# One encoder block on one core: moving four small pieces of work between engines and within their queues

## The chip, the cores and the metric

The kernel runs on one core of one Trainium2 chip. The metric is the device time of one execution in microseconds (us). A core has TensorE (PE in the profile; its weight loads are listed apart, as PEld), VectorE (DVE), ScalarE (ACT), GpSimd (POOL) and SyncE (SP, which here only issues transfers). Each engine works through its own list of instructions in order. An instruction that has to wait for another engine holds up everything behind it on its own engine.

## The reference

The block computes, for 1024 tokens and 16 meta tokens put ahead of them (1040 columns in all), in float32:

```
h = h + mixer(rms_norm(h));  h = h + swiglu(rms_norm(h));  return rms_norm(h)[:, 16:]

mixer(h): q, k, v of branch A and of branch B and two gates are columns of h @ w_in
  branch A, per head (4):  s1 = q1 k1' * scale - slope * |i - j|   (meta keys have distance 0)
                           s2 = q2 k2' * scale - slope * |i - j|
                           y  = (softmax(s1) - lam * softmax(s2)) @ v, then rms_norm
  branch B: attention in a window of 128, with sinks
  merged = sigmoid(ga) * (y_a @ w_ba) + sigmoid(gb) * (y_b @ w_bb);  return merged @ w_o
```

## The kernel before

A float32 product is made of three matmuls on operands that are split into a high and a low part (`split`, lines 123 to 126: ACT makes the high part, DVE or POOL the low one). The large products use a scheme with 7 instead of 8 block products. The program goes through these stages: norms and projections with branch B's attention between them (to about 270 us), branch A's attention (270 to 590 us), the merge of the branches (from 603 us), the output product, and the feed-forward part (to the end). The change lies in branch A's attention and at the beginning of the merge.

**Branch A's attention** is a loop over 32 tiles (4 heads of 8 tiles of 128 query rows, numbered n = 0 to 31 here), with one more pass for what is left over. For each tile, `scores_a` makes two score maps of 128 x 1040, first m = 1, then m = 0. For each map PE multiplies in three chunks (line 1051): two of 352 columns into the two banks of the tile `two`, which has one buffer, and one of 336 into a bank of the tag `sc`, of which there are three. DVE reads the first two chunks in one instruction (line 1054), adding the distance and taking the row minimum, and then the third (line 1058). That one reads its distances from `far_m`, one of three small buffers that POOL fills by a copy from `dist` (`far_copy`, line 1001), one buffer for each tile in turn. ACT takes the exponential of a map (line 1062). DVE makes the reciprocal of a sum (1065), a factor (1067), and the combined map s1 - factor * s2 (1068, over 1040 columns). Behind that, line 1070 on DVE copies the 16 meta columns twice more to the right of the map (32 columns), because the value product later takes them in several roles.

One pass later `transpose_a` turns the map in three groups of blocks (b = 0, 1, 2; PE line 1080 into `sc` banks, ACT line 1083 and DVE line 1084 out of them; b = 2 is the group with the meta columns). `values_a` multiplies by the values (line 1093), and `normed_a` ends every fourth tile with a norm: its sums (line 1106) and its factors turned on PE (line 1117).

**The gates** run in the gaps of the attention. `gate_steps` yields after every three matmuls (line 938; three are called a quarter here, four quarters make one block product). The weights of a block product are made by POOL (`weights_g`, lines 817 to 837: up to two additions, then a cast at 836 and a subtraction at 837) into four buffers, four block products ahead. A buffer is free when PE has finished the block product that used it. Each result leaves PSUM by ACT or DVE (lines 945 to 977). The last column of gates (k = 7) has its block products p = 5, 7, 3, 4 last in the program; p = 4 goes on in the bank that p = 7's result has just been read from (line 970).

**The order on PE is written by hand.** A string of letters says what each pass does in turn: s is the next piece of scores (two chunk pieces and the last chunk for each map, six in all), t the next group of transposes, g one gate quarter, n the next piece of values or norm. Tiles from n = 16 on use `"ssgsgnssgtsgntgnt"`. For n % 4 = 3 the first n of that string is one of the empty waiting steps of `normed_a` (`N_WAIT`), so that there is no work in it. The other engines' orders come from a scheduler, which weighs readiness; `tc.issue_after(x)` makes it put what is inside behind x in order.

**At the merge** the results of branch B are loaded, and `split_yb` makes their high and low parts: `yb0` and `yb1` first (`ybpool`), then `yb2` and `yb3` (`ybpool2`), on ACT and DVE. Then come the products with `w_bb` (`branch_w` loads and splits their weights, line 742; the matmuls are at 750). Parts of `w_out`, 1 MB each, are loaded by `load_wo` (line 1340) in the same stretch.

Of the kernel before, what the change touches and what calls it, by code (L numbers as in the profile page):

```python
# [19 lines left out]
P = 128  # L20
# [6 lines left out]
NT = S // P  # L27
# [16 lines left out]
FAR_LATE = 6  # L44
LAST_B = ("T1", 4), (5, "V0"), (5, "T2"), ("T2", 6), (7, "V1"), (7, "V2")
SLOTS_LAST = "ggggntgntnt"
S_BUFS = (2, 2)
AT_BUFS = 2
G_BUFS = 3
# [29 lines left out]
def encoder_block(ctx: ExitStack, tc: tile.TileContext, x, meta, norm_mix, w_in, lq1, lk1, lq2, lk2,  # L79
# [656 lines left out]
    close_psum1()  # L736


    def branch_w(p, o, src, nme, raw=None, low=None, tag="wh"):
        w = (raw_tile(f"wbr{nme}_{o}")[:, 0:512] if raw is None else raw).rearrange("p (c n) -> p c n", n=P)  # L740
        if raw is None:
            nc.sync.dma_start(w, src[:, o * P:(o + 1) * P].rearrange("(c p) n -> p c n", p=P))
# [108 lines left out]
    def turn_into(i):  # L851
# [16 lines left out]
        if i == 2:  # L868
            for late in raws_g[4:]:
                queue_behind([late], last)  # L870

    def gate_steps():
        banks, kept = {}, {}

# [36 lines left out]
        for n, (k, p) in enumerate(order_g):  # L911
# [23 lines left out]
            for c in range(4):  # L935
# [6 lines left out]
                if c == 3:  # L942
# [18 lines left out]
                    elif p == 6:  # L961
                        u = kept.pop(k)
                        add(u, ps, u, ALU.add)
                        held_stores.append((u_d[k], u))
                    elif p == 5:
                        kept["q"] = kept_g(f"q_{k}")
                        nc.scalar.copy(kept["q"], ps)
                    elif p == 7:
                        st = stage_g(f"g22_{k}")
                        add(st, ps, kept.pop("q"), ALU.add)  # L970
# [25 lines left out]
    def far_copy(n):  # L996
        if n < AH * NT:
            with ExitStack() as after:
                if 2 < n < FAR_LATE:
                    after.enter_context(tc.issue_after(made_g[-1].ins))  # L1000
                nc.gpsimd.tensor_copy(far_m[n % 3][:, 0:S - 704], dist[:, 1600 - n % NT * P:1600 - n % NT * P + S - 704])

# [29 lines left out]
    def scores_a(h, t, ld, s):  # L1032
# [8 lines left out]
        u0 = 896 - t * P  # L1041
        far = far_m[(h * NT + t) % 3]
        for m in (1, 0):
            if m == 0:
                far_copy(h * NT + t + 2)
            s[m] = s0s[t % 2] if m == 0 else apool.tile([P, L], F32, tag="s1", name=f"as1_{nm}", bufs=S_BUFS[1])
            two = psum2.tile([P, 2, 512], F32, tag="two", name=f"aps2_{nm}_{m}", bufs=1)
            for i, (k0, n) in enumerate(A_CHUNKS):
# [18 lines left out]
        nc.vector.tensor_scalar(dn[:, 0:1], first_sum, dn[:, 1:2], neglam, ALU.mult, ALU.mult)  # L1067
        nc.vector.scalar_tensor_tensor(s[0][:, 0:L], s[1][:, 0:L], dn[:, 0:1], s[0][:, 0:L], ALU.mult, ALU.add)
        more, last = s[0][:, L:L + 2 * NM].rearrange("p (a k) -> p a k", a=2), s[0][:, S:L].unsqueeze(1).broadcast_to([P, 2, NM])
        nc.vector.scalar_tensor_tensor(more, last, 1.0, last, ALU.mult, ALU.max)  # L1070

    def transpose_a(h, t, s, at_):
        i = t % 2
# [85 lines left out]
    for n in range(AH * NT + T_LAG):  # L1159
# [30 lines left out]
            scoring = scores_a(h, t, ld, s)  # L1190
        if n >= T_LAG:
            turning = turn(tiles[n - T_LAG])
        for what in SLOTS[n % 2 if n < 2 * NT else 2] if n < AH * NT else SLOTS_LAST:
            if what == "s":
                next(scoring, None)
            elif what == "t":
# [54 lines left out]
    while n_made[0] < len(order_g):  # L1251
        fill(1)
    close_gwork()
    ybpool2, close_yb2 = pool("ybpool2")
    split_yb(ybpool2, 2)
    order_pe.__exit__(None, None, None)
    fill(1000)
    close_psum2()
    close_psumg()
    close_stage()  # L1260
# [95 lines left out]
    for o in range(DC):  # L1356
# [602 lines left out]
```

## Time and profile before

| | |
|---|---|
| median of 3 runs | 1411.83 us (1411.62 to 1412.45) |
| the profiled execution, its own time | 1410.71 us |
| its span, first to last instruction | 1408.9 us |
| outside the span | 1.81 us |
| PE busy | 1397.5 us, 99% of the span |
| DVE, ACT, POOL busy | 939.9, 673.9, 665.6 us |
| matmuls | 7171 |

A row of the trace's timeline gives the start of a group of equal instructions in us from the beginning of the span, the time from its start to the end of its last one, engine, line, operation, tiles (what is written, an arrow, what is read), shapes and count; in brackets stands the idle time of the engine ahead of it and what ended that. The matmuls of PE overlap in the trace: one of 512 columns is shown for 0.39 us, and the next starts 0.23 us after it. A stall shows in the distance of two starts, and only the part of it above 0.39 us is idle time of PE. A row of the waits gives who waited for whom, the total in us, how often, and the longest.

### The profile page before, as it was taken

What the parts mean: (1) busy time and instruction counts of PE and PEld (TensorE: products, weight loads), DVE (VectorE), ACT (ScalarE), POOL (GpSimd) and SP (SyncE); (2) the same over time, 40 slices, a digit from 0 to 9 for tenths busy, and PEclk for the clock granted to TensorE, in tenths of its full rate; (3) what the DMA queues carried; (4) which work ended last, traced back from release to release, by engine and by line L of the source; (5) the groups of instructions that cost most, each with busy time, mean ns of one, the idle gap of its engine ahead of it and who ended that gap; (6) DMA issues with size and microseconds to landing.
All of it is one profiled execution on the core that took longest, in us unless ns stands there. A gap on an engine that the chain in (4) does not pass through costs nothing.

```text
span 1408.9 us, 20675 instructions
## 1 busy us (share of the span) xinstructions
PE 1397.5 (99%) x7171; PEld 1199.4 (85%) x7171; DVE 939.9 (67%) x1619; ACT 673.9 (48%) x1285; POOL 665.6 (47%) x634
## 2 busy tenths in 40 slices
PE   9999999999999999999999999999999999999998
PEld 8989999888888888888888888888888888888886
DVE  6556667677677878767968956544455443887566
ACT  6356565545454555554446644333333333444454
POOL 4156885577777776523404055544444441000442
PEclk9999999999999999999999999999999999999999
DMA  8446658564886363495613634433233222954333
GB/s 238 91 123 181 199 177 295 148 194 155 266 286 221 109 202 107 140 323 160 202 43 120 187 110 139 133 112 110 96 101 108 102 99 107 367 181 141 120 126 146
DMA packets 193016, 227.73 MB, mean 162 GB/s; under 512 B 16952, under 2 KB 126464, under 8 KB 192784
## 3 DMA queue, kind: packets, MB, share of 16 engines
q1 hardware_dynamic: 190160, 222.80, 48.5%
q10 hardware_dynamic: 2752, 3.61, 0.8%
q8 instruction: 56, 0.92, 0.3%
q14 instruction: 48, 0.39, 0.1%
HBM read 152.48 MB, written 68.39 MB: 157 GB/s over the span
## 4 chain that ended last, share of the span: by engine, by line
PE 92%; DVE 4%; ACT 2%; issue 1%; POOL 1%; DMA 0%; SPq 0%; ACTq 0%; DVEq 0%; POOLq 0%
PE pg L1722 30%; PE pd L1826 15%; PE pg L938 9%; PE ppa L750 6%; PE po L1625 4%; PE aps L1051 3%; PE pp_va L236 3%; PE pp_ka L236 3%; PE pp_qb L236 3%; PE apy L1093 2%; PE bps L416 2%; PE pp_qa L236 2%; PE po L1633 2%; PE apt L1080 2%; PE bpy L463 1%; PE bpt L457 1%
## 5 line engine op out<-in xcount | busy, mean ns | idle before, releaser
L1722 PE MATMUL pg<-t,wop 128*128 128x512 f32 x1056 | 242.4, 389 | 0.0
L1722 PEld LDWEIGHTS pg<-t,wop 128*128 128x128 f32 x1056 | 198.2, 188 | 41.2
L125 POOL TENSOR_TENSOR wop<-wf,wop 128x512 fp32r<-128x512 f32 x114 | 151.2, 1326 | 164.8 <-ACT wop L124 152.8
L1826 PE MATMUL pd<-ob,oa 128*128 128x512 f32 x924 | 209.6, 389 | 0.0
L1826 PEld LDWEIGHTS pd<-ob,oa 128*128 128x128 f32 x924 | 173.4, 188 | 36.0
L938 PE MATMUL pg<-hT_hi,wopg 128*128 128x512 f32 x488 | 183.0, 401 | 0.8 <-POOL wopg L837 0.6
L1722 PE MATMUL pg<-b,wop 128*128 128x512 f32 x792 | 183.3, 389 | 0.0
L1722 PEld LDWEIGHTS pg<-b,wop 128*128 128x128 f32 x792 | 148.4, 188 | 30.7
L1062 ACT ACTIVATE as<-as,amn 128x1040 f32<-128x1040 f32 x64 | 74.6, 1166 | 99.5 <-DVE amn L1058 99.5
L124 ACT ACTIVATE wop<-wf 128x512 fp32r<-128x512 f32 x128 | 80.8, 632 | 73.3 <-PE pg L1722 49.7
L125 POOL TENSOR_TENSOR oa<-ra,oa 128x512 fp32r<-128x512 f32 x27 | 34.9, 1294 | 168.6 <-ACT oa L124 167.2
L938 PEld LDWEIGHTS pg<-hT_hi,wopg 128*128 128x128 f32 x488 | 91.5, 188 | 15.6 <-POOL wopg L837 1.1
L124 ACT ACTIVATE oa<-ra 128x512 fp32r<-128x512 f32 x77 | 48.7, 632 | 108.1 <-PE pd L1826 50.1
L938 PE MATMUL pg<-hT_lo,wopg 128*128 128x512 f32 x244 | 95.8, 393 | 0.0
L1499 DVE TENSOR_TENSOR s<-wf,wf 128x512 f32<-128x512 f32 x22 | 15.5, 704 | 111.2 <-DMA wf<-in_w_ff_up_dram 70.5
L1051 PE MATMUL aps<-ak,aq 128*128 128x352 f32 (+1 forms) x384 | 87.1, 335 | 1.9 <-DVE amn L1054 1.2
L1051 PEld LDWEIGHTS aps<-ak,aq 128*128 128x128 f32 x384 | 63.0, 189 | 11.8 <-DVE amn L1054 5.5
L1054 DVE CUSTOM_DVE_ANT_0 as<-aps,dist,far_a 128x704 f32<-128x704 f32 x64 | 60.3, 942 | 15.6 <-PE aps L1051 15.4
L418 DVE CUSTOM_DVE_ANT_0 bs<-bps,tbx,nsink 128x432 f32<-128x432 f32 (+1 forms) x64 | 38.5, 628 | 47.2 <-PE bps L416 32.6
L428 POOL TENSOR_SCALAR bs<-bs,bdn 128x432 f32<-128x432 f32 (+1 forms) x64 | 37.0, 596 | 51.9 <-DVE bdn L426 29.4
L1749 ACT COPY p<-pg 128x512 f32<-128x512 f32 x44 | 25.8, 587 | 66.5 <-PE pg L1722 66.5
L1093 PEld LDWEIGHTS apy<-at,av 128*128 128x128 f32 x400 | 54.0, 189 | 4.1
(340 smaller groups left out, 3164.1 us busy)
## 6 DMA issues: line engine op xcount, KB each, us to landing
ra<-aop SPq DMA_DIRECT2D x77, 256.0 KB, 2.6
wf<-in_w_ff_gate_dram SPq DMA_DIRECT2D x25, 512.0 KB, 3.7
wf<-in_w_ff_up_dram SPq DMA_DIRECT2D x25, 512.0 KB, 3.6
aop<-as SPq DMA_DIRECT2D x44, 256.0 KB, 2.1
wg_s<-in_w_in_dram SPq DMA_DIRECT2D x18, 512.0 KB, 4.5
aop<-c SPq DMA_DIRECT2D x33, 256.0 KB, 2.0
ak<-ka_d SPq DMA_DIRECT2D x16, 520.0 KB, 6.2
t_d<-tst SPq DMA_DIRECT2D x16, 512.0 KB, 4.5
```

Source lines behind the costliest of these rows:

```text
L124: high = nc.scalar.activation(hi, src, AF.Copy)
L125: lo_eng.tensor_tensor(lo, src, f32(hi), ALU.subtract)
L236: product = nc.tensor.matmul(ps[:, :n], a[:, c, :], b[:, c, at:at + n], start=(u == 0), stop=(u == 3 * DC - 1))
L750: nc.tensor.matmul(ps, w[:, a, j, :], src(j, b, tk), start=(j == 0 and n == 0), stop=(j == 3 and n == 2))
L938: product = nc.tensor.matmul(ps, op[:, x, c, :], h[:, 4 * d + c, HALF[t]], start=(p in (1, 6, 7) and c == 0 and i == 0), stop=(p in (2, 6, ...
L1051: nc.tensor.matmul(ps[:, :n], qs[m][:, t * P:(t + 1) * P], ks[m][:, vv, k0:k0 + n], start=(vv == 0), stop=(vv == 1))
L1054: nc.vector.tensor_tensor_reduce(s[m][:, 0:2 * n].rearrange("p (a k) -> p a k", a=2), two[:, :, :n], dist[:, u0:u0 + 2 * n].rearrange("p ( ...
L1062: nc.scalar.activation(s[m][:, 0:L], s[m][:, 0:L], AF.Exp, bias=mn[:, m, 1:2], scale=-1.0, accum_out=dn[:, 1:2] if m else first_sum)
L1093: nc.tensor.matmul(py[:, cols], v[:kp, a, k, :], at_[:kp, k, b, :], start=(k == 0 and j == 0), stop=(k == 8))
L1625: nc.tensor.matmul(sets_o[p][u], oa[:, a, u * P:(u + 1) * P], ob[:, b, :], start=(p in (1, 5) and j == 0 and k == 0), stop=(p in (2, 3) an ...
L1722: nc.tensor.matmul(ps, op[:, x, c, :], b[:, y, c, :], start=(p in (1, 5) and c == 0 and n == 0), stop=(p in (4, 2, 3) and c == 3 and n == ...
L1826: nc.tensor.matmul(ps[u], oa[:, a, u * P:(u + 1) * P], ob[:, b, :], start=(p in (1, 2, 5) and j == 0 and k == 0), stop=(p in (2, 3, 4) and ...
```

## The change

1. **Meta columns.** The copy of the 32 columns (line 1070) is no longer a `scalar_tensor_tensor` on DVE but a `copy` on ACT.
2. **Distance copies.** `far_copy` for tile n + 2 is called at the end of tile n, no longer between its two maps, and every copy from the fourth on is put in order behind the last gate weight that POOL was given by then (before, that held for three of them only).
3. **Fourth tiles.** Tiles 19, 23, 27 and 31 have an order string of their own, in which one gate quarter that stood behind the second map's two chunks stands ahead of them.
4. **Branch B's last parts.** The rest of the gates is written ahead of the split of `yb2` and `yb3`, and that split is put behind the addition that empties the last p = 7 bank. Three of the loads of `w_out` are put behind loads of `w_bb`.

```
+SLOTS_3 = "ssgsgngsstsgntgnt"
...
-            nc.sync.dma_start(w, ...)
+            w_loads[nme, o] = nc.sync.dma_start(w, ...)
...
-                        add(st, ps, kept.pop("q"), ALU.add)
+                        sums_g[k] = add(st, ps, kept.pop("q"), ALU.add)
...
-                if 2 < n < FAR_LATE:
+                if n > 2:
                     after.enter_context(tc.issue_after(made_g[-1].ins))
                 nc.gpsimd.tensor_copy(far_m[n % 3][:, 0:S - 704], dist[...])
...
         for m in (1, 0):
-            if m == 0:
-                far_copy(h * NT + t + 2)
...
-        nc.vector.scalar_tensor_tensor(more, last, 1.0, last, ALU.mult, ALU.max)
+        nc.scalar.copy(more, last)
+        far_copy(h * NT + t + 2)
...
-        for what in SLOTS[n % 2 if n < 2 * NT else 2] if n < AH * NT else SLOTS_LAST:
+        for what in (SLOTS_3 if n % 4 == 3 and n >= 2 * NT else SLOTS[n % 2 if n < 2 * NT else 2]) if n < AH * NT else SLOTS_LAST:
...
     close_gwork()
+    fill(1000)
     ybpool2, close_yb2 = pool("ybpool2")
-    split_yb(ybpool2, 2)
+    with tc.issue_after(sums_g[7].ins):
+        split_yb(ybpool2, 2)
     order_pe.__exit__(None, None, None)
-    fill(1000)
...
         if 3 <= o < 6:
-            load_wo(*((w11, 0, 0), (w12, 0, 1), (w21, 1, 0))[o - 3])
+            with tc.issue_after(w_loads["b", o].ins):
+                load_wo(*((w11, 0, 0), (w12, 0, 1), (w21, 1, 0))[o - 3])
```

Line numbers in the rows below are those of each kernel by itself: in the changed one they are 3 to 6 higher around here (line 938 is 943 there, 1054 is 1057, 1058 is 1061, 1062 is 1065, 1068 is 1071, 1080 is 1084, 1084 is 1088).

PE in tile 19, from the last chunk of its first map to the last chunk of its second (`aps` are scores, `pg` a gate quarter, `apt` the transposes), before:

```order
L1051 MATMUL aps_3_1_5571<-ak_1_5229,aq_1_5228 128x336 x2
L938 MATMUL pg_5_5481<-hT_hi,wopg_5_5391 128x512
L938 MATMUL pg_5_5481<-hT_lo,wopg_5_5391 128x512
L938 MATMUL pg_5_5481<-hT_hi,wopg_5_5391 128x512
L1051 MATMUL aps_2_3_0_5581<-ak_0_5234,aq_0_5233 128x352 x4
L938 MATMUL pg_5_5481<-hT_hi,wopg_5_5391 128x512
L938 MATMUL pg_5_5481<-hT_lo,wopg_5_5391 128x512
L938 MATMUL pg_5_5481<-hT_hi,wopg_5_5391 128x512
L1080 MATMUL apt_2_0_5592<-ident,as_0_3435 128x128 x4
L1051 MATMUL aps_3_0_5599<-ak_0_5234,aq_0_5233 128x336 x2
```

And now:

```order
L1054 MATMUL aps_3_1_5571<-ak_1_5229,aq_1_5228 128x336 x2
L943 MATMUL pg_5_5481<-hT_hi,wopg_5_5391 128x512
L943 MATMUL pg_5_5481<-hT_lo,wopg_5_5391 128x512
L943 MATMUL pg_5_5481<-hT_hi,wopg_5_5391 128x512 x2
L943 MATMUL pg_5_5481<-hT_lo,wopg_5_5391 128x512
L943 MATMUL pg_5_5481<-hT_hi,wopg_5_5391 128x512
L1054 MATMUL aps_2_3_0_5585<-ak_0_5234,aq_0_5233 128x352 x4
L1084 MATMUL apt_2_0_5591<-ident,as_0_3435 128x128 x4
L1054 MATMUL aps_3_0_5598<-ak_0_5234,aq_0_5233 128x336 x2
```

Three matmuls of a gate have moved from behind the second map's four matmuls to ahead of them, and the transposes follow these directly. PE's order differs at the same place of tiles 23, 27 and 31, and nowhere else.

DVE from the combined map of tile 27 to the first map of tile 28 (`as_1` is the map of tile 27; the bare rows of 128x1 read a minimum out), before:

```order
L1068 SCALAR_TENSOR_TENSOR as_1_3436<-as_3_3_6351,adn_3_6350,as_1_3436 128x1040
L1084 TENSOR_TENSOR at_2_6262<-apt_2_1_6410,at_2_6262 128x4x128
L1084 TENSOR_TENSOR at_2_6262<-apt_2_2_6432,at_2_6262 16x128
L1070 SCALAR_TENSOR_TENSOR as_1_3436<-as_1_3436 128x32
L1054 ISA as_3_4_6443,amn_4_6440<-aps_3_4_1_6444,dist,far_a 128x704
L1054 ISA amn_4_6440 128x1
```

And now:

```order
L1071 SCALAR_TENSOR_TENSOR as_1_3436<-as_3_3_6351,adn_3_6350,as_1_3436 128x1040
L1088 TENSOR_TENSOR at_2_6262<-apt_2_1_6409,at_2_6262 128x4x128
L1088 TENSOR_TENSOR at_2_6262<-apt_2_2_6431,at_2_6262 16x128
L1057 ISA as_3_4_6443,amn_4_6440<-aps_3_4_1_6444,dist,far_a 128x704
L1057 ISA amn_4_6440 128x1
```

The copy of the meta columns has gone from ahead of the next tile's first map, and the rest stands as it was. On ACT it stands now behind the last eviction of the transposes of tile 26 and ahead of the first exponential of tile 28:

```order
L1087 ACTIVATE at_2_6262<-apt_2_1_6409 128x4x128
L972 COPY q_6419<-pg_5_6301 128x512
L1087 ACTIVATE at_2_6262<-apt_2_2_6431 128x128
L1073 COPY as_1_3436<-as_1_3436 128x32
L1065 ACTIVATE as_3_4_6443,adn_4_6441<-as_3_4_6443,amn_4_6440 128x1040
L1087 ACTIVATE at_2_6262<-apt_3_0_6486 128x4x128
```

POOL in tiles 15 to 17 (`wopg` are gate weights being made, `far_m` with the numbers 3431, 3432 and 3433 are the three distance buffers), before:

```order
L836 CAST wopg_3_5072<-wg_s_0_4692 128x512
L837 TENSOR_TENSOR wopg_3_5072<-wg_s_0_4692,wopg_3_5072 128x512
L836 CAST wopg_4_5127<-wg_s_1_4690 128x512
L1001 COPY far_m_3431<-dist 128x320
L837 TENSOR_TENSOR wopg_4_5127<-wg_s_1_4690,wopg_4_5127 128x512
L824 TENSOR_TENSOR s1g_5172<-wg_s_1_4922 128x512
L836 CAST wopg_5_5174<-s1g_5172 128x512
L837 TENSOR_TENSOR wopg_5_5174<-s1g_5172,wopg_5_5174 128x512
```

And now:

```order
L840 TENSOR_TENSOR wopg_3_5071<-wg_s_0_4692,wopg_3_5071 128x512
L1006 COPY far_m_3432<-dist 128x320
L839 CAST wopg_4_5127<-wg_s_1_4690 128x512
L840 TENSOR_TENSOR wopg_4_5127<-wg_s_1_4690,wopg_4_5127 128x512
L827 TENSOR_TENSOR s1g_5171<-wg_s_1_4922 128x512
L839 CAST wopg_5_5173<-s1g_5171 128x512
L840 TENSOR_TENSOR wopg_5_5173<-s1g_5171,wopg_5_5173 128x512
L1006 COPY far_m_3433<-dist 128x320
```

Before, the copy for tile 18 (buffer 3431) stands between a weight's cast and its subtraction. Now the copies for tiles 16 and 17 stand around this stretch, each behind a finished weight; the copy for tile 18 comes 13 gate instructions later than it did.

More of the change, by code (lines that the diff above doesn't have):

```diff
@@ L736, in encoder_block @@
     close_psum1()
+    w_loads = {}
     def branch_w(p, o, src, nme, raw=None, low=None, tag="wh"):
@@ L741, in branch_w @@
         if raw is None:
-            nc.sync.dma_start(w, src[:, o * P:(o + 1) * P].rearrange("(c p) n -> p c n", p=P))
+            w_loads[nme, o] = nc.sync.dma_start(w, src[:, o * P:(o + 1) * P].rearrange("(c p) n -> p c n", p=P))
         wh = p.tile([P, 2, 4, P], F32R, tag=tag, name=f"wbh{nme}_{o}", bufs=WB_BUFS)
@@ L870, in turn_into @@
                 queue_behind([late], last)
+    sums_g = {}
     def gate_steps():
```

## The prediction

> **What bounds the kernel now.** First the page's engine line, then the busy times in stretches of the span.
>
> ```profile
> PE 1397.5 (99%) x7171; PEld 1199.4 (85%) x7171; DVE 939.9 (67%) x1619; ACT 673.9 (48%) x1285; POOL 665.6 (47%) x634
> ```
>
> ```profile
> 360.00:450.00 90.00, 89.36 (x527) 79.16 (x527) 67.90 (x148) 42.44 (x79) 70.07 (x66) 1.00 0.78 257
> 450.00:530.00 80.00, 79.49 (x491) 70.58 (x489) 66.05 (x149) 43.19 (x78) 58.59 (x57) 1.00 0.47 154
> 530.00:583.00 53.00, 51.10 (x316) 44.71 (x316) 46.12 (x102) 27.70 (x51) 33.45 (x31) 1.00 0.30 99
> ```
>
> PE is the bound, and no edit takes a matmul away. So the change can be worth only what PE stalls. In branch A's attention, where most of it lies, PE is idle for 0.64, 0.51 and 1.90 us of these three stretches (length less the first busy time): 3.05 us. DVE is the next engine, 46.12 of 53.00 us at the worst. A stall costs more than its idle time, since the end of the matmul ahead of it covers part. The waits of PE's weight loads name the releaser:
>
> ```profile
> PEld aps L1051 <- DVE amn L1054: 5.5, 9, 1.2
> ```
>
> The scores of a map wait for DVE to have read the map before out of `two`. I take the stalls one by one, by the distance of two starts.
>
> **The change part by part.**
>
> *Fourth tiles.* The first of the four (tile 19), and the last (tile 31):
>
> ```profile
> 466.12 0.39 PE L938 MATMUL pg<-hT_lo,wopg 128*128 128x512 f32 x1
> 466.36 0.40 PE L938 MATMUL pg<-hT_hi,wopg 128*128 128x512 f32 x1
> 466.76 0.07 DVE L1054 DVE_READ_ACCUMULATOR2_ANT amn<- 128x1 f32 x1
> 466.88 0.90 PE L1051 MATMUL aps<-ak,aq 128*128 128x352 f32 x4
> ...
> 572.56 0.40 PE L938 MATMUL pg<-hT_hi,wopg 128*128 128x512 f32 x1
> 573.09 0.92 PE L1051 MATMUL aps<-ak,aq 128*128 128x352 f32 x4
> ```
>
> Gate matmuls start 0.24 us apart (466.12, 466.36); then 0.52 us pass to the second map's scores, which start 0.12 us after DVE's readout. Tile 31 loses the same (573.09 - 572.56 = 0.53). So four tiles lose about 0.3 us each: **1.2 us**. A quarter put ahead is three matmuls, 3 x 0.23 = 0.69 us, more than the 0.3 that DVE is late; the wait goes. What is late next: the second map starts 0.69 - 0.3 = 0.39 us later, and its readers on DVE with it. But its last chunk follows now without a quarter between and comes 0.3 us earlier, so the second reader (1058) is bound only by the first. The bare adjacency costs or gains up to 0.1 us a tile: a run of four scores takes 0.90 us in the rows above, and 0.80 us where its weights were loaded in time:
>
> ```profile
> 280.51 0.80 PE L1051 MATMUL aps<-ak,aq 128*128 128x352 f32 x4
> ```
>
> I take nothing for it, and 0.4 us either way for the range.
>
> *Meta columns.* Five stalls stand behind line 1070. Tiles 18 and 22:
>
> ```profile
> 457.38 0.97 DVE L1070 SCALAR_TENSOR_TENSOR as<-as 128x32 f32<-128x32 f32 x1
> 458.83 0.40 PE L938 MATMUL pg<-hT_hi,wopg 128*128 128x512 f32 x1
> 459.28 0.91 PE L1051 MATMUL aps<-ak,aq 128*128 128x352 f32 x4
> ...
> 491.11 0.78 DVE L1070 SCALAR_TENSOR_TENSOR as<-as 128x32 f32<-128x32 f32 x1
> 492.22 0.40 PE L938 MATMUL pg<-hT_hi,wopg 128*128 128x512 f32 x1
> 492.81 0.91 PE L1051 MATMUL aps<-ak,aq 128*128 128x352 f32 x4 [0.20 <-DVE amn L1054]
> ```
>
> Two starts are 0.45 and 0.59 us apart in place of 0.23: 0.22 and 0.36 us. The copy is 0.97 and 0.78 us long there, more than the loss, and 1054, whose readout frees `two`, is queued right behind it (as the rows of 546.56 and 547.68 show for tile 28). Then tiles 27 and 28:
>
> ```profile
> 537.77 1.27 DVE L1070 SCALAR_TENSOR_TENSOR as<-as 128x32 f32<-128x32 f32 x1
> 540.79 0.60 PE L1117 MATMUL apf<-ident,af 128*128 128x128 f32 x4
> 541.15 0.57 DVE L1058 CUSTOM_DVE_ANT_0 as<-aps,far_m,amn 128x336 f32<-128x336 f32 x1
> 541.78 0.66 PE L1080 MATMUL apt<-ident,as 128*128 128x128 f32 x4 [0.40 <-DVE amn L1058]
> 543.45 2.40 DVE L1068 SCALAR_TENSOR_TENSOR as<-as,adn,as 128x1040 f32<-128x1040 f32 x1
> 546.39 1.31 POOL L837 TENSOR_TENSOR wopg<-s1g,wopg 128x512 fp32r<-128x512 f32 x1
> 546.49 1.23 PE L1093 MATMUL apy<-at,av 128*128 128x256 f32 x9
> 546.56 1.19 DVE L1070 SCALAR_TENSOR_TENSOR as<-as 128x32 f32<-128x32 f32 x1
> 547.68 0.93 DVE L1054 CUSTOM_DVE_ANT_0 as<-aps,dist,far_a 128x704 f32<-128x704 f32 x1
> 548.67 0.91 PE L1051 MATMUL aps<-ak,aq 128*128 128x352 f32 x4 [0.96 <-DVE amn L1054]
> ...
> 575.98 0.60 PE L1117 MATMUL apf<-ident,af 128*128 128x128 f32 x4
> 576.71 0.66 PE L1080 MATMUL apt<-ident,as 128*128 128x128 f32 x4
> ```
>
> Nine value matmuls are 0.12 us apart, (1.23 - 0.28) / 8 with the last one's 0.28; PE was ready at 546.49 + 9 x 0.12 = 547.57 and began at 548.67: 1.10 us. Without the copy 1054 starts at 546.56, 1.12 us earlier: gone. Four turns are 0.11 us apart, so PE was ready at 541.23 and went on at 541.78: 0.55 us, and tile 31 in the same way at 576.42 and 576.71: 0.29 us. There the transposes wait for the second map's 1058, which had been pushed back by the 1.27 us copy in the first map. The five come to 0.22 + 0.36 + 1.10 + 0.55 + 0.29 = 2.5 us. The last two lie in fourth tiles, whose second map now starts 0.39 us later, so I leave 0.2 us there: **2.3 us**.
>
> Why the copy is so long there: its median is 0.31 us and its longest 1.27, and the one of 546.56 ends (547.75) just behind the POOL subtraction that had begun ahead of it (547.70).
>
> ```profile
> L1070 DVE SCALAR_TENSOR_TENSOR as<-as x32: 169/310/1275, 286.1 to 580.8; 128x32 f32<-128x32 f32 x32
> L1083 ACT ACTIVATE at<-apt 128x128 fp32r<-128x128 f32 x32 | 8.9, 277 | 7.4 <-PE apt L1080 7.3
> ```
>
> On ACT the trace shows no copy of 32 columns. Its nearest row is an eviction of 128 columns at 0.277 us: 32 x 0.277 = 8.9 us more work at most, nothing at least. ACT is busy 113.33 of 223.00 us in the three stretches (42.44 + 43.19 + 27.70), so idle time takes it. It waits there for the combined map (1068), with the next tile's exponential queued behind it. That exponential needs DVE's reading of the next map, which stands behind 1068 on DVE in any case, so the wait adds nothing. I cost it at 0; were ACT's cover gone, it is the 8.9 us.
>
> By the Trainium skill, page "SBUF — State Buffer", section "Who interferes with whom", DVE and GpSimd share a port pair as an exclusive lock, a DVE instruction with two SBUF inputs contends with a GpSimd one that reads SBUF, and ACT never waits. The pair of rows at 546.39 and 546.56 agrees. The rule also speaks against the change: 1068 has two SBUF inputs and stays on DVE, and a POOL that waits less gets in its way at other places. By the rule as it helps, the sum is the one below; as it hurts, it is the first rival.
>
> *Distance copies.* In tile 15 POOL waits 3.5 us for DVE ahead of a copy, and the weights behind it come late:
>
> ```profile
> 432.12 0.46 POOL L1001 COPY far_m<-dist 128x320 f32<-128x320 f32 x1 [3.52 <-DVE amn L1058]
> 437.07 0.40 PE L938 MATMUL pg<-hT_lo,wopg 128*128 128x512 f32 x1
> 438.10 0.73 PE L938 MATMUL pg<-hT_hi,wopg 128*128 128x512 f32 x2 [0.64 <-POOL wopg L837]
> ```
>
> PE loses 438.10 - 437.07 - 0.23 = **0.8 us**. Put behind a tile's maps, the copy finds its buffer free, and POOL has the 3.5 us for the weights.
>
> *Branch B's last parts.* DVE takes a split of `yb` ahead of the addition that frees the last bank:
>
> ```profile
> 599.93 0.68 DVE L970 TENSOR_TENSOR g<-pg,q 128x512 f32<-128x512 f32 x1
> 600.25 0.97 PE L938 MATMUL pg<-hT_hi,wopg 128*128 128x512 f32 x2
> 601.07 0.39 PE L938 MATMUL pg<-hT_lo,wopg 128*128 128x512 f32 x1
> ```
>
> Two steps take 0.82 us in place of 0.46: **0.36 us**, which goes when the addition comes first. The four splits behind it, 0.68 us each by that row for the same shape, fit ahead of the first product that needs them, some 3 us on. The loads of `w_out` change places with loads of `w_bb`; PE has no wait in the merge, so I cost that at 0.
>
> **The sum:** 1.2 + 2.3 + 0.8 + 0.36 = 4.7 us. I take 0.5 us off for new collisions on DVE, half of one stall like that of 547.57, since 1068 was drawn out there too (2.40 us). That leaves **4.2 us**: 1410.71 - 4.2 = 1406.5 for an execution like the profiled one, and with the median 1.12 us above it, 1407.6.
>
> **The rivals.**
>
> *Collisions come back.* POOL's weights shift in time, 1068 is drawn out elsewhere, and DVE is as late as before. Against: the copy's own collisions are gone from DVE for good. For: 2.40 us at 543.45. Then the 1.2 and 2.3 us are halved by new stalls, and 0.8 + 0.36 stay, less one stall of 1.1: 1411.83 - 1.8 = 1410.0.
>
> *The wait moves within the fourth tiles.* The transposes of 541.78 wait for the second map's 1058, and all four second maps come 0.39 us later. If 1058 is bound by that, the four tiles lose 4 x 0.39 = 1.6 us there: 1411.83 - 4.2 + 1.6 = 1409.2. Against: the last chunk comes earlier now, and only two of the four tiles showed that wait.
>
> *Slower: a distance copy comes late.* Its place is POOL's queue: each copy stands now behind a finished weight. That for tile 20 stands behind the weight whose subtraction ends at 471.61, and its reader starts at 475.50:
>
> ```profile
> 470.32 1.29 POOL L837 TENSOR_TENSOR wopg<-wg_s,wopg 128x512 fp32r<-128x512 f32 x1
> 475.50 0.57 DVE L1058 CUSTOM_DVE_ANT_0 as<-aps,far_m,amn 128x336 f32<-128x336 f32 x1 [0.17 <-DVE amn L1054]
> ```
>
> That leaves 3.9 us, less 0.46 us for the copy. It decides once POOL is over 3.4 us later than now; from there each us holds DVE, and PE with it. Half a us on each of the 16 tiles of heads 2 and 3 is 8 us: 1411.83 - 4.2 + 8 = 1415.6. Against: POOL loses 3.5 us waits of the kind shown at 432.12, so it should be earlier.
>
> **How the numbers follow.** The forecast, 1407.6 (by itself 1405.8 to 1409.0: 1.3 us and the 0.5 us allowance below, 1.4 above), has 0.66. The moved wait has 0.12, the collisions 0.15, the late copies 0.07. That the edits do not take place is ruled out by the orders shown. The range goes from 1405.8 to 1411.0; it takes in both mild rivals and leaves out the late copies and the tails. A measurement of this kernel can tell about 0.2%, 2.8 us, from no change, so faster means below 1409.0: nearly all of the forecast (0.62) and 0.05 of the moved wait make 0.67. Within 0.2%: the rest of these two (0.11) and the collisions, 0.26. Slower: 0.07.
>
> **What would show it.** In the changed kernel's trace the starts of second scores in tiles 19, 23, 27 and 31 follow the gate matmul by 0.23 us; DVE has no 32-column instruction, ACT 32 more of under 0.28 us; POOL's wait for 1058 ahead of `far_m` (many us) is gone; PE has no wait for `wopg` and none at the last p = 4. The weight loads' wait of 5.5 us should fall below 1.5 us. Wrong would be: that wait as long as before at other places, 1058 waiting for POOL, or ACT's exponentials later behind the copies.

## The result, and the profile after

| | before | changed |
|---|---|---|
| median, first set (6 and 6 executions) | 1411.72 us | 1407.24 us (1405.37 to 1409.17) |
| ratio, first set | | 0.9967, 95% interval 0.9954 to 0.9980 |
| median, second set (17 and 5) | 1411.73 us | 1405.91 us (1404.94 to 1408.36) |
| ratio, second set | | 0.9958, 95% interval 0.9944 to 0.9972 |
| span of the profiled execution | 1408.9 us | 1407.4 us |
| first score starts on PE | 277.48 us | 281.35 us |
| last gate matmul starts on PE | 603.37 us | 601.18 us |
| stretch between the two | 325.89 us | 319.83 us |

The change is 4.5 us faster in the first set and 5.8 us in the second; 4.2 were forecast. The last row is the sharpest measure of it, since the places where PE's order differs and all the stalls that the prediction lists lie between these two matmuls. In the changed kernel lines 938, 1051, 1054, 1058, 1068 and 1080 are 943, 1054, 1057, 1061, 1071 and 1084, and the copy of the meta columns is 1073. These are the changed kernel's engine line and the same three stretches as in the prediction (length, then PE, PEld, DVE, ACT and POOL busy):

```profile
PE 1395.9 (99%) x7171; PEld 1200.2 (85%) x7171; DVE 921.3 (65%) x1587; ACT 680.0 (48%) x1317; POOL 658.8 (47%) x634
```

```profile
360.00:450.00 90.00, 90.00 (x536) 80.37 (x535) 64.00 (x142) 45.01 (x88) 70.43 (x69) 1.00 0.84 275
450.00:530.00 80.00, 80.00 (x499) 72.31 (x498) 63.28 (x141) 44.77 (x88) 53.05 (x53) 1.00 0.46 150
530.00:583.00 53.00, 53.00 (x337) 47.95 (x337) 42.58 (x98) 30.66 (x63) 38.73 (x35) 1.00 0.32 101
```

PE is busy in every microsecond of the three stretches, where before it was idle for 3.05 us. The stalls went one by one where they were looked for. First tile 19, where the prediction showed the rows of 466.12 to 466.88:

```profile
468.50 0.93 DVE L1057 CUSTOM_DVE_ANT_0 as<-aps,dist,far_a 128x704 f32<-128x704 f32 x1
...
469.37 0.07 DVE L1057 DVE_READ_ACCUMULATOR2_ANT amn<- 128x1 f32 x1
469.44 0.39 PE L943 MATMUL pg<-hT_lo,wopg 128*128 128x512 f32 x1
...
469.67 0.40 PE L943 MATMUL pg<-hT_hi,wopg 128*128 128x512 f32 x1
469.90 0.32 PE L1054 MATMUL aps<-ak,aq 128*128 128x352 f32 x1
```

The second map's scores follow the gate matmul by 0.23 us; DVE's readout had ended at 469.44, 0.46 us ahead. Then tile 28, where before one stall had cost 1.10 us:

```profile
544.18 1.29 DVE L1071 SCALAR_TENSOR_TENSOR as<-as,adn,as 128x1040 f32<-128x1040 f32 x1
544.30 1.64 POOL L839 CAST wopg<-s1g 128x512 fp32r<-128x512 f32 x1
...
545.50 0.22 ACT L1073 COPY as<-as 128x32 f32<-128x32 f32 x1 [0.51 <-DVE as L1071]
...
546.19 0.93 DVE L1057 CUSTOM_DVE_ANT_0 as<-aps,dist,far_a 128x704 f32<-128x704 f32 x1
...
546.85 1.23 PE L1097 MATMUL apy<-at,av 128*128 128x256 f32 x9
...
547.92 0.81 PE L1054 MATMUL aps<-ak,aq 128*128 128x352 f32 x4
```

Nine value matmuls of 0.12 us after 546.85 come to 547.93, and the scores start at 547.92. **Two** things differ from before on DVE: the 32-column copy is gone from ahead of the first map's reader (546.19), and the combined map takes 1.29 us in place of 2.40. The second was no part of the forecast, and it is what the experiments below turn on. In before, POOL's addition began 0.01 us behind the map (543.45 in the prediction's rows):

```profile
543.46 1.29 POOL L824 TENSOR_TENSOR s1g<-wg_s 128x512 f32<-128x512 f32 x1
```

In the changed kernel POOL's cast begins 0.12 us behind the map, and it is the cast that is drawn out (1.64 us; 0.61 us alone).

POOL's waits, first of before, then of the changed kernel, each from 283 to 605 us:

```profile
POOL far_m L1001 <- DVE amn L1058: 57.7, 25, 5.4
POOL wopg L836 <- PE pg L938: 13.7, 5, 4.8
POOL av L1021 <- PE apy L1093: 3.9, 2, 2.0
POOL af L1112 <- DVE af L1111: 3.4, 4, 1.4
```

```profile
POOL af L1116 <- DVE af L1115: 35.1, 8, 9.2
POOL wopg L839 <- PE pg L943: 20.8, 10, 4.9
POOL av L1026 <- PE apy L1097: 18.9, 3, 7.6
```

POOL waits no longer for the second map, but it waits about as long in sum as before, now for the norms (1116), for `av` and for free weight buffers (839). These waits cost PE nothing: it has no wait for `wopg` left.

The profiled execution of the changed kernel reached the first score late. Both rows are PE's, of before and of the changed kernel:

```profile
277.48 0.32 PE L1051 MATMUL aps<-ak,aq 128*128 128x352 f32 x1
```

```profile
281.35 0.33 PE L1054 MATMUL aps<-ak,aq 128*128 128x352 f32 x1
```

That is 3.87 us, in front of all that the change moves. It and 0.65 us behind the last gate matmul hide most of the 6.06 us won in the stretch, and the span shows only 1.5 us of gain. Whether the late start belongs to the change had to be tested. The 0.65 us do not follow the edits: the part behind the last gate matmul is 805.56 us of the span in before and 806.20 here, but 805.63 in two variants of the changed kernel below that keep its fourth edit, and 806.05 in the kernel before with the order string alone.

### The profile page after: what moved, and what is told of

The parts are those of the page before. It is cut to its first block, busy times and chain, and to the rows that moved or that the text cites. A ratio compares the mean times of both kernels' runs of the same rounds, so it can differ in the third digit from the quotient of the medians.

```text
span 1407.4 us, 20700 instructions
## 1 busy us (share of the span) xinstructions
PE 1395.9 (99%) x7171; PEld 1200.2 (85%) x7171; DVE 921.3 (65%) x1587; ACT 680.0 (48%) x1317; POOL 658.8 (47%) x634
## 3 DMA queue, kind: packets, MB, share of 16 engines
q1 hardware_dynamic: 190160, 222.80, 49.5%
## 4 chain that ended last, share of the span: by engine, by line
PE 92%; DMA 3%; DVE 1%; issue 1%; ACT 1%; SPq 1%; POOL 0%; ACTq 0%; DVEq 0%; POOLq 0%
PE pg L1728 30%; PE pd L1832 14%; PE pg L943 12%; PE ppa L753 6%; PE aps L1054 4%; PE po L1631 4%; PE apy L1097 3%; PE pp_va L237 3%; PE pp_ka L237 2%; PE apt L1084 2%; PE pp_qa L237 2%; PE pp_qb L237 2%; PE po L1639 2%; PE bps L417 1%; PE bpy L464 1%; PE bpt L458 1%
```

## The experiments

**One edit at a time on the kernel before.** The first four kernels shared the runs of before (median 1411.74 us, 33 executions). The first:

```
-        nc.vector.scalar_tensor_tensor(more, last, 1.0, last, ALU.mult, ALU.max)
+        nc.scalar.copy(more, last)
```

> The kernel before with one edit: the meta columns copied by ScalarE. The changed kernel's trace has no PE stall behind the old DVE copy, and two stalls are gone that the prediction did not list (tiles 26 and 30, 0.24 and 0.22 us at 530.27 and 565.48 of before). Theory 1, each edit removes its own stalls: PE's stretch from the first score to the last gate matmul falls from 325.9 us by 2.5 to 3.4 us (3.4 if the stalls of tiles 26 and 30 are the copy's too), the median to 1408.3 to 1409.2; the fourth tiles keep 0.3 us each and POOL its wait of some 58 us for the second map. Rival, the collisions move on: 1068 is drawn out in other places, the stretch falls by less than 1 us, the median is 1410.7 or more.

Measured: 1408.38 us (11 executions), ratio 0.9979 (0.9970 to 0.9988), the stretch 322.83 us: **3.06 us** less. All seven stalls behind the copy are gone, those of tiles 26 and 30 too, so these two were the copy's as well. Theory 1 holds, but the rival's mechanism is there: 1068 takes 54.5 us in sum, 5.1 more than before, and makes two new stalls, of 0.16 and 0.45 us. The second in this kernel's timeline (1068 is the combined map):

```profile
480.31 2.43 DVE L1068 SCALAR_TENSOR_TENSOR as<-as,adn,as 128x1040 f32<-128x1040 f32 x1
480.35 1.29 POOL L826 TENSOR_TENSOR wg_s<-wg_s,wg_s 128x512 f32<-128x512 f32 x1
...
484.45 0.75 PE L1051 MATMUL aps<-ak,aq 128*128 128x352 f32 x3 [0.29 <-DVE amn L1054]
```

The combined map, 1.29 us when undisturbed, is drawn out to 2.43 beside a POOL addition of 1.29 us, and PE waits at 484.45. At tile 28 the map is drawn out here too (2.41 us at 542.10), but without the copy behind it PE does not stall.

Which of the two is drawn out turns on hundredths of a microsecond. Over the 14 traces of this study, a POOL addition or subtraction of 128x512 that began with the combined map or up to 0.03 us behind it kept its length of about 1.3 us, and the map took 2.39 to 2.43; one that began 0.06 to 0.22 us behind it took 2.25 to 2.40 us itself, and the map 1.29 to 1.30. So any edit that shifts POOL or DVE by a tenth of a microsecond can make such a collision or take it away.

The second, with the distance copies alone:

```
-                if 2 < n < FAR_LATE:
+                if n > 2:
...
-            if m == 0:
-                far_copy(h * NT + t + 2)
...
+        far_copy(h * NT + t + 2)
```

> The kernel before with one edit: the distance copies behind a tile's maps. Theory 1: POOL's 58 us of waiting for the second map are gone, the 0.8 to 0.9 us stall for the gate weights at 437.07 goes, and the stretch falls by 0.9 us (325.0), the median to 1410.8. Rival, POOL's shifted subtractions hit DVE's copies at other places: the stalls behind line 1070 change by over 1 us in sum, either way, so that the stretch is above 326.0 or below 324.0.

Measured: 1408.80 us (11), ratio 0.9979 (0.9970 to 0.9988), the stretch 323.18: **2.71 us** less, three times the forecast. The stall of 437.07 went as foreseen (0.80 us and 0.11 behind it). But those of 541.23 and 547.57 went too, with the copy still on DVE, and so did those of tiles 22, 26 and 30 (0.36, 0.24 and 0.22 us). Of the seven, only tiles 18 (0.22) and 31 (0.30) keep theirs. The rows of tile 28 in this kernel (1066 is the combined map, 1068 the copy, 1049 the scores):

```profile
544.02 1.29 DVE L1066 SCALAR_TENSOR_TENSOR as<-as,adn,as 128x1040 f32<-128x1040 f32 x1
...
546.03 1.19 DVE L1068 SCALAR_TENSOR_TENSOR as<-as 128x32 f32<-128x32 f32 x1
...
546.98 1.23 PE L1092 MATMUL apy<-at,av 128*128 128x256 f32 x9
...
548.15 0.75 PE L1049 MATMUL aps<-ak,aq 128*128 128x352 f32 x3
```

The copy is as long as before (1.19 us) and the stall is 0.1 us: the combined map was not drawn out, since POOL's next operation began 0.12 us behind it (544.14) and not 0.01. Two new stalls, of 0.37 and 0.44 us, stand elsewhere. The rival is right here; what POOL does at that moment decides.

The third, with the order string alone:

```
+SLOTS_3 = "ssgsgngsstsgntgnt"
...
-        for what in SLOTS[n % 2 if n < 2 * NT else 2] if n < AH * NT else SLOTS_LAST:
+        for what in (SLOTS_3 if n % 4 == 3 and n >= 2 * NT else SLOTS[n % 2 if n < 2 * NT else 2]) if n < AH * NT else SLOTS_LAST:
```

> The kernel before with one edit: the gate quarter ahead of the second scores in the fourth tiles. Theory 1: four times 0.3 us, the stretch falls by 1.2 us (324.7), the median to 1410.5, and the stalls of tiles 27 and 31 at the transposes (0.55 and 0.29 us) stay. Rival, the wait moves within the tiles: with the meta copy still on DVE the later second map makes the transposes of all four tiles wait for 1058, and the stretch falls by less than 0.4 us (325.5 or more), the median is 1411.3 or more.

Measured: 1408.97 us (11), ratio 0.9980 (0.9971 to 0.9989), the stretch 323.59: **2.30 us** less, more than theory 1 or its rival had. The four waits went, 0.30 us each. Also gone are 541.23, 547.57 and tile 26's 0.24 us; but at transposes of fourth tiles a new stall of 0.54 us stands (504.42), and the one of tile 31 has grown from 0.29 to 0.69 us (575.16). Here are both effects in this kernel (copy 1071, combined map 1069, second reader 1059, transposes 1081):

```profile
500.81 0.87 DVE L1071 SCALAR_TENSOR_TENSOR as<-as 128x32 f32<-128x32 f32 x1
...
503.79 0.57 DVE L1059 CUSTOM_DVE_ANT_0 as<-aps,far_m,amn 128x336 f32<-128x336 f32 x1
...
504.42 0.66 PE L1081 MATMUL apt<-ident,as 128*128 128x128 f32 x4 [0.39 <-DVE amn L1059]
```

```profile
542.97 2.41 DVE L1069 SCALAR_TENSOR_TENSOR as<-as,adn,as 128x1040 f32<-128x1040 f32 x1
...
546.97 0.31 DVE L1071 SCALAR_TENSOR_TENSOR as<-as 128x32 f32<-128x32 f32 x1
547.09 0.75 PE L1052 MATMUL aps<-ak,aq 128*128 128x352 f32 x3
```

In tile 28 now the map is drawn out (2.41) and the copy isn't (0.31), and again PE doesn't wait. So the 1.10 us stall of before needed both extensions, 1.1 us on the map and 1.0 us on the copy: in each of these three kernels one of the two is missing, and at most 0.1 us of the stall is left.

The fourth, with the last parts of branch B alone:

```
     close_gwork()
+    fill(1000)
     ybpool2, close_yb2 = pool("ybpool2")
-    split_yb(ybpool2, 2)
+    with tc.issue_after(sums_g[7].ins):
+        split_yb(ybpool2, 2)
     order_pe.__exit__(None, None, None)
-    fill(1000)
```

> The kernel before with one edit: the splits of the last parts of branch B behind the addition that frees the last gate bank (the order of the loads of w_out stays as before). Theory 1: the 0.36 us at 600.25 go, the stretch falls by 0.3 to 0.4 us (325.5), the median to 1411.4. Rival, the splits are late for the merge now: the stretch falls but PE's part behind the last gate matmul (799.2 us) grows as much, and the median is 1411.7 as before.

Measured: 1411.19 us (11), ratio 0.9994 (0.9986 to 1.0003), the stretch 325.62: 0.27 us less, and 0.28 us at the place itself; PE's part behind the last gate matmul is 799.23 us against 799.21. Theory 1 by the trace; the median cannot tell so small a gain from none. The other stalls of before stand in this second execution within 0.05 us of their sizes (1.14 us at 548.08, 0.80 at 437.69): they repeat from run to run.

**Undoing one edit in the changed kernel.** The next four shared a chip (before: 1411.73 us, 17 executions). First the meta copy back on DVE (the first diff above, reversed):

> The changed kernel with the meta copy put back on DVE, so with the other three edits alone. Theory 1 (the simple sum): it loses what the edit alone had brought, 3.1 us of PE's stretch from the first score to the last gate matmul (319.8 + 3.1 = 322.9), and the median is 1410.3. Theory 2 (the stalls of 541, 547 and 576 us were alignments of POOL's subtractions with the copy, and any of the three edits moves POOL or the maps enough to lose them): only the stalls of the third tiles come back (0.22 + 0.36 + 0.24 + 0.22, and 0.1 each for the scores behind, 1.4 us in sum), and one or two new ones at the transposes of fourth tiles (0.5 to 0.7 us each, as in the kernel with the slots alone): the stretch is 321.3 to 322.4, the median 1408.7 to 1409.8.

Measured: 1406.95 us (6), ratio 0.9965 (0.9953 to 0.9978), the stretch 321.61. **The simple sum fails:** the edit that gave 3.06 us alone is worth 1.8 us against the first profile of the changed kernel and 1.0 us against the second (below). Theory 2 holds in kind, not in place: of the third tiles' stalls one came back (0.22 us), two stand at transposes of fourth tiles, of 0.93 and 0.40 us, and one of 0.22 us in tile 2. The larger one in this kernel:

```profile
498.75 1.29 POOL L827 TENSOR_TENSOR s1g<-wg_s 128x512 f32<-128x512 f32 x1
...
498.82 1.26 DVE L1073 SCALAR_TENSOR_TENSOR as<-as 128x32 f32<-128x32 f32 x1
...
501.43 0.60 PE L1121 MATMUL apf<-ident,af 128*128 128x128 f32 x4
...
502.81 0.44 PE L1084 MATMUL apt<-ident,as 128*128 128x128 f32 x2 [0.79 <-DVE amn L1061]
```

POOL's addition began 0.07 us ahead of the copy; the copy ends (500.08) just behind it (500.04). The delay runs through both maps to the transposes. This is the prediction's second rival, set off here by the copy on DVE. By the medians alone this kernel cannot be told from the changed one (1406.01 to 1407.96 us, and 1404.94 to 1408.36 in the second set); the 1.8 and 1.0 us rest on one profile of this kernel.

Then the changed kernel once more, unchanged:

> The changed kernel once more, unchanged. Its first profiled execution reached the first score 3.87 us later than that of before (281.35 against 277.48), though no engine's order differs ahead of it. Theory 1, the time ahead of the first score varies from execution to execution: this profile has it at another place between 277 and 282 us, the stretch from the first score to the last gate matmul is again 319.8 within 0.2 us, and the median over the rounds is 1406.5 to 1407.5. Rival, the changed program is slower there as compiled: the first score is again at 281 us or later.

Measured: 1405.91 us (5), 0.6 us under the forecast's range, the first score at 279.90, the stretch 320.58. The first score stands at another place again, as theory 1 has it, and over all 14 profiles of this study it lies between 277.44 (the changed kernel with the meta copy on DVE) and 281.35 us. The changed kernel with one edit undone reached 277.44, 278.82 and 277.68. So the late start belongs to the execution, not to the change; the order of PE's, DVE's and ACT's instructions ahead of the first score is the same in all 14. The stretch missed the forecast of 319.8 within 0.2 by 0.6 us, through one stall of 0.45 us in tile 2 and the scores behind it:

```profile
296.50 1.30 POOL L820 TENSOR_TENSOR wg_f<-wg_f 128x512 f32<-128x512 f32 x1 [2.36 <-DMA wg_f<-in_w_in_dram]
...
296.72 2.17 DVE L1071 SCALAR_TENSOR_TENSOR as<-as,adn,as 128x1040 f32<-128x1040 f32 x1
...
300.42 0.75 PE L1054 MATMUL aps<-ak,aq 128*128 128x352 f32 x3 [0.21 <-DVE amn L1057]
```

A weight load landed later in this execution, POOL's addition started just ahead of the combined map, and the map took 2.17 us in place of 1.42. This is the first rival at its real price.

The old order of the fourth tiles (`SLOTS` in place of `SLOTS_3`):

> The changed kernel with the old order of the fourth tiles. Theory 1: the four waits of 0.30 us for the readout of line 1054 are back and nothing else, the stretch is 319.8 + 1.2 = 321.0, the median 1408.4. Rival (alignments): with other places for POOL's subtractions a drawn-out combination (1068) adds 0.2 to 0.5 us at one or two places, as with the meta copy alone; the stretch is 321.2 to 322.0, the median up to 1409.4.

Measured: 1407.87 us (9), ratio 0.9974 (0.9964 to 0.9983), the stretch 321.94. Four waits of 0.30 us are back, and with them one of 0.34 us at 484.64 and the 0.45 us in tile 2: the rival in size, though the stall in tile 2 was there in the second profile of the changed kernel too.

The distance copies at their old place (the second diff, reversed):

> The changed kernel with the distance copies at their old place. Theory 1: POOL waits some 50 us for the second maps again, the 0.8 us stall for the gate weights at about 437 us is back with 0.1 behind it, and nothing else: the stretch is 319.8 + 0.9 = 320.7, the median 1408.1. Rival (alignments): a second stall for late weights or a drawn-out 1068 adds 0.5 us or more, the stretch is 321.2 or more.

Measured: 1407.81 us (9), ratio 0.9975 (0.9965 to 0.9985), the stretch 322.67. The stall for the weights is back (0.79 us at 438.29), and five more, of 0.45, 0.25, 0.16, 0.44 and 0.35 us: the rival again. The last of them is the moved wait at the transposes of a fourth tile (tile 23), with the copy on ScalarE:

```profile
503.73 0.57 DVE L1063 CUSTOM_DVE_ANT_0 as<-aps,far_m,amn 128x336 f32<-128x336 f32 x1
...
504.36 0.66 PE L1085 MATMUL apt<-ident,as 128*128 128x128 f32 x4 [0.20 <-DVE amn L1063]
```

In sum:

| edit | alone on before, stretch | undone in the changed kernel, stretch (against its two profiles) |
|---|---|---|
| meta columns | -3.06 us | +1.8, +1.0 us |
| distance copies | -2.71 us | +2.8, +2.1 us |
| fourth tiles | -2.30 us | +2.1, +1.4 us |
| branch B's last parts | -0.27 us | not tried |
| all four | -8.34 us summed; -6.06 and -5.31 us measured | |

**What the copy waits for.** Of the 32 copies of before, each one longer than 0.2 us ends 0.04 to 0.05 us behind the end of a POOL instruction that had begun ahead of it; those of 0.17 to 0.18 us found POOL idle or within 0.13 us of its end, began up to 0.06 us ahead of its next instruction, or met a very small one (128x4). Two kernels ask whether it must be so on DVE. One puts a plain copy in the same place of the kernel before:

```
-        nc.vector.scalar_tensor_tensor(more, last, 1.0, last, ALU.mult, ALU.max)
+        nc.vector.tensor_copy(more, last)
```

> The kernel before, with its meta copy still on DVE and at its place, but as a plain copy with one input in place of the operation with two. In the traces of before and of the changed kernel with the copy back on DVE, every copy longer than 0.2 us ends 0.04 to 0.05 us behind a POOL instruction that had begun ahead of it, and copies that begin ahead of POOL take 0.17 to 0.18 us. Theory 1 (the lock is one of the second input, as the Trainium skill, page SBUF — State Buffer, section Who interferes with whom, has it): all 32 copies take 0.2 us or less, the stalls behind them go as with the copy on ScalarE, the stretch from the first score to the last gate matmul is 322.6 to 323.3 us, the median 1408.2 to 1408.9. Rival (any DVE copy in the memory waits for POOL): the lengths reach 1.2 us again and the stretch is 325.9.

Measured: 1411.62 us (11; before 1411.85 of 21), ratio 1.0000 (0.9991 to 1.0009), the stretch 325.87. The rival: the plain copy waits for POOL as long as the operation with two inputs, so having one input does not spare it the wait. The other has a reduction over one element there, which also copies:

```
-        nc.vector.scalar_tensor_tensor(more, last, 1.0, last, ALU.mult, ALU.max)
+        nc.vector.tensor_reduce(more.unsqueeze(3), last.unsqueeze(3), AX.X, ALU.max)
```

> The kernel before, with its meta copy still on DVE and at its place, but as a reduction (a maximum over one element), which has one input. The plain copy with one input had waited for POOL just as the operation with two. By the Trainium skill, page SBUF — State Buffer, section Who interferes with whom, a copy can run in a mode that takes both ports and then contends, a reduction can not. Theory 1, it is the second port that waits: all 32 reductions take 0.2 us or less, the stalls behind them go, the stretch from the first score to the last gate matmul is 322.6 to 323.4 us and the median 1408.2 to 1408.9. Rival, any DVE instruction that reads the memory here waits for POOL's running instruction: lengths reach 1.2 us as before, the stretch is 325.9, the median 1411.7.

Measured: 1407.67 us (8; before 1411.64 of 12), ratio 0.9969 (0.9959 to 0.9980), the stretch 321.47: **4.42 us** less by another operation on the same engine, more than the 3.06 us of the copy on ScalarE alone (one profile each; the intervals of the ratios overlap). The trace's answers for the line, as shortest, median and longest in ns, of the plain copy and of the reduction (the operation of before had 169/310/1275):

```profile
L1070 DVE COPY as<-as x32: 158/306/1274, 287.8 to 582.4; 128x32 f32<-128x32 f32 x32
```

```profile
L1070 DVE TENSOR_REDUCE as<-as x32: 162/169/186, 288.9 to 578.9; 128x32 f32<-128x32 f32 x32
```

In 26 of its 32 places a POOL instruction was running when the reduction began, and none waited. The four fourth-tile waits of 0.30 us are all that is left up to 580 us. The stall at 437.07 is gone too, which ScalarE's copy alone had left there (0.79 us). By the Trainium skill, page "SBUF — State Buffer", section "Who interferes with whom", a plain copy can run in a mode that uses the shared port pair and then contends with GpSimd, and a reduction never does; the two rows agree. Why the reduction's stretch is shorter than with ScalarE's copy is not settled by a run: the combined map took 54.5 us in sum with ScalarE's copy and 49.5 with the reduction, so other alignments are likely, the stall for the weights among them.

**The cover on ScalarE.** The changed kernel with each copy made four times:

```
-        nc.scalar.copy(more, last)
+        for _ in range(4):
+            nc.scalar.copy(more, last)
```

> The changed kernel with the meta copy on ScalarE made four times in place of once, which is 96 copies or 96 x 0.22 = 21 us more work on ScalarE in the attention, so that its cover is tested. Theory 1, ScalarE has idle time and PE waits for DVE alone: the stretch from the first score to the last gate matmul is 319.8 to 320.6 as without, the median 1405.9 to 1407.2. Rival, the exponentials or evictions behind the copies come late by 0.66 us a tile and PE with them: 10 us or more, the median 1416.

Measured: 1405.61 us (5), ratio 0.9953 (0.9941 to 0.9966), the stretch 319.76, no stall in the tiles: theory 1. 21 us more work on ScalarE costs nothing that can be measured.

**The slower case.** The changed kernel with each distance copy one tile later (tile 1's is then made twice):

```
-        far_copy(h * NT + t + 2)
+        far_copy(h * NT + t + 1)
```

> The changed kernel with each distance copy ordered one tile later, so that it tests the slower case of the prediction. In the changed kernel the copies end 4.0 us (tile 20) to 21.5 us ahead of their reader on DVE, seven of them less than 10 us (tiles 3, 11, 12, 13, 19, 20, 21). Theory 1, a copy that is late holds DVE and PE: one tile is 8.3 to 9.5 us, so tile 20's copy is some 4 to 5 us late and the others up to 2; the stretch grows by 4 to 10 us from 319.8, with DVE waits for POOL's distance copy, and the median is 1411 to 1417. Rival, POOL's order ahead of the readers is loose enough: the waits move onto POOL's slack, the stretch stays within 1 us, the median at 1407.

Measured: 1413.36 us (11; before 1411.85), ratio 1.0009 (1.0000 to 1.0018), the stretch 327.20, 7.4 us longer: theory 1 in size. How it comes about is not what was expected. DVE hardly waits for POOL (0.2 us in all); instead the scheduler has put the late readers further back in DVE's list. Tiles 19 and 20 of the changed kernel, copy and first reader of each:

```profile
461.18 0.45 POOL L1006 COPY far_m<-dist 128x320 f32<-128x320 f32 x1
...
469.62 0.57 DVE L1061 CUSTOM_DVE_ANT_0 as<-aps,far_m,amn 128x336 f32<-128x336 f32 x1 [0.17 <-DVE amn L1057]
...
473.55 0.45 POOL L1006 COPY far_m<-dist 128x320 f32<-128x320 f32 x1
...
477.98 0.56 DVE L1061 CUSTOM_DVE_ANT_0 as<-aps,far_m,amn 128x336 f32<-128x336 f32 x1
```

And tile 19 of this one, from its copy to its first reader (471.46 is where DVE reads the tile's first two chunks):

```profile
471.46 0.94 DVE L1057 CUSTOM_DVE_ANT_0 as<-aps,dist,far_a 128x704 f32<-128x704 f32 x1
...
473.32 0.44 POOL L1006 COPY far_m<-dist 128x320 f32<-128x320 f32 x1
...
475.32 0.62 PE L1121 MATMUL apf<-ident,af 128*128 128x128 f32 x4 [0.50 <-DVE at L1088]
...
476.73 0.66 PE L1084 MATMUL apt<-ident,as 128*128 128x128 f32 x4 [0.78 <-DVE yg L1122]
...
478.66 0.56 DVE L1061 CUSTOM_DVE_ANT_0 as<-aps,far_m,amn 128x336 f32<-128x336 f32 x1
```

The changed kernel's reader starts 0.17 us behind the read of the first two chunks. Here it starts 6.3 us behind it, and 4.9 us behind its finished copy, after other work, and PE waits for that work at 475.32 and 476.73. Left at its old place it would have waited 1.4 us for its copy (473.76, against 472.40). The cost is one of order, paid without a wait that names the copy. That PE waits because the unread chunks keep `sc` banks occupied is likely from the code, where 1121 and 1084 write into the same three banks, and was not tested.

## Why the prediction was right, point by point

- **The bound and the places** were right. What PE stalled was all there was to win, and the weight loads' wait of 5.5 us for line 1054 has left no row in the first profile of the changed kernel.
- **Fourth tiles, 1.2 us:** four times 0.30 us in the trace, and nothing for the bare adjacency. Right.
- **Meta columns, 2.3 us:** each listed stall went, for 2.44 us (0.22, 0.36, 0.51, 1.12, 0.23). Two of the kind were overlooked, tiles 26 and 30, 0.46 us together; and behind five of the stalls the run of scores is 0.11 us shorter, 0.53 us, which only the fourth tiles' paragraph had considered. So the term was 3.4 us, not 2.3.
- **The step that failed** is the sum, which gives each stall to one edit. Those of 541.23, 547.57 and 576.42, 1.9 us in all, went with the copy; the first two also went with the distance copies alone and with the order string alone. The row of 543.45 (2.40 us) was read as a warning of new collisions, when it was half of the largest stall. For all four edits together it made no difference which edit took them. For a single edit the working would have been off by up to a factor of three (2.71 us for the distance copies against 0.8 forecast, 2.30 for the order string against 1.2).
- **Distance copies, 0.8 us:** 0.92 at the place itself. **Branch B, 0.36 us:** 0.28.
- **ScalarE at 0:** right. The copy takes 0.22 us there, within the bounds of 0 and 0.28, and even four of them cost nothing.
- **The 0.5 us for new collisions:** none in the first profile, 0.45 us in the second. Right in size. With one edit undone the kernel shows up to five new stalls.
- **The terms add to 5.8 us** (1.19 + 2.44 + 0.46 + 0.53 + 0.92 + 0.28) where 4.7 stood, and the two profiles give 6.06 and 5.31 us of stretch. The median of the first set moved by 4.5 us; that it lies so close to the forecast is in part luck, since one execution differs from the next by up to 4 us ahead of the first score. The second set's 5.8 us fits the terms. The forecast was somewhat low.
- **The rivals.** Collisions: real, 0.2 to 0.5 us each in the changed kernel's relatives. The moved wait: real at two of the four fourth tiles, 0.4 to 0.9 us with the copy on DVE, and 0.35 us at one of them with the copy on ScalarE and the distance copies at their old place. The changed kernel has none. The late copy: the changed kernel's copy for tile 20 ends 3.99 us ahead of its reader (3.4 was estimated), and one tile less costs 7.4 us, though through DVE's order and not through the wait that was foreseen.

## What to carry to other kernels

Stalls made by two drawn-out instructions in a row belong to neither alone: before a stall is booked to an edit, look at every instruction in its chain that is longer than its own shortest, and expect edits that share such a stall to sum to less than their parts. Beside a busy POOL, look for a form of a very short DVE operation that does not wait for POOL: here a reduction over one element never took more than 0.19 us and a copy on ScalarE never more than 0.23, while a plain copy on DVE took up to 1.27. Where single executions vary by as much as the change is worth, time the stretch between two fixed matmuls that enclose it.

## What was not expected of the hardware

The 32-column copy lasts until POOL's running weight operation ends: 0.17 us alone, up to 1.27 us beside a subtraction of 1.29 us, with one input or two, and 0.16 to 0.19 us always as a reduction. With the same order of PE's, DVE's and ACT's instructions ahead of it, the first score came at any place between 277.4 and 281.4 us, through waits ahead of it that differ between executions, while the stalls within the attention repeated within 0.05 us (but for one of 0.45 us behind a load that landed late). Not tried: the changed kernel with the reduction in place of ScalarE's copy, and the changed kernel without the fourth edit. By its stretch the changed kernel is the fastest of those run, but for its variant with the copies made four times, which can't be told from it; by the medians neither the changed kernel with the meta copy on DVE nor the kernel before with the reduction can be told from it with certainty.
